# Split matmuls that run from the last column to the first, and logits of two heads in turn, in a decoder trunk

## The chip, the core and the metric

The kernel runs on one core of a Trainium2 chip. The metric is the device time of one execution in microseconds. The core has a matmul engine (TensorE, PE in the profile, with its weight loads shown apart as PEld), VectorE (DVE), ScalarE (ACT), GpSimd (POOL) and SyncE (SP), which here issues the large transfers from HBM.

## What is computed

A decoder trunk of two layers on 256 tokens of width 1024, all in float32. Layer 0 mixes by causal pooling, then a dense SwiGLU of width 2816. Layer 1 is a dilated sliding-window attention, then a top-2-of-8 expert SwiGLU of width 3584. Cut to what matters:

```python
h = h + pool_mixer(rmsnorm(h, a_norm[0]), a_proj[0], a_scale[0])
hn = rmsnorm(h, ffn_norm[0])
h = h + (silu(hn @ dense_w_gate) * (hn @ dense_w_up)) @ dense_w_down
kv = rmsnorm(h, kv_norm) @ w_kv                  # keys and values, 3 groups x 16 heads x 64
q = rmsnorm(h, b_norm[0]) @ w_q
logits = einsum('brnqhd,brnkhd->brnhqk', qs, kb) * HEAD_DIM ** -0.5 + bias   # per group, in its dilated window
...                                              # softmax over the three groups' keys together
h = h + merged @ w_o
xf = rmsnorm(h, ffn_norm[1])
...                                              # the two best of 8 experts for each token
ys = (silu(xb @ moe_w_gate[e]) * (xb @ moe_w_up[e])) @ moe_w_down[e]
h = h + gate * ys
return rmsnorm(h, final_norm)
```

## The kernel before

**Split matmuls.** Every large matmul takes float32 operands that are cut in two numbers of the type fp32r, a high part and a low part. ScalarE writes the high part `wh` of a weight piece as a copy to fp32r (line 178), VectorE subtracts it from the raw weights to give the low part `wl` (L182). The helper `mm3` then makes three matmuls for each 128 rows of the contraction: high by high and high by low (L190), and low by high (L193), all into one PSUM tile. With `weights_first` the weight piece is the stationary operand and 256 tokens are the moving one (gate, up and down of the dense layer, and the keys and queries). Without it the activations are stationary and the moving operand is a piece of the weights, 256 columns wide for the values and 512 for the output projection and the experts. The profile names the operands with the moving one first or last, by the program's names, and gives shapes as stationary and moving.

From the loops, the program runs 3312 split matmuls of 256 moving columns (1584 in the dense layer, 1728 for keys, queries and values) and 4104 of 512 (4008 in the experts, 96 in the output projection). The scatter of the experts' results (`scatter`, L1070 and L1071, 64 matmuls of 512 columns) uses fp32r operands too, but doesn't go through `mm3`. The last piece of the last expert (`native_unit`, L1042), the transposes, the gathers and the attention itself are plain float32 matmuls, each of which the profile shows as two records.

**Attention.** It runs in four blocks `b` of four heads. In each block come the projections of keys and queries, then the values, each cut into steps of 24 split matmuls. The queries and keys of a pair of heads, 2j and 2j+1, lie in one tile, the even head on partitions 0 to 63 and the odd one on 64 to 127. For each head `h` and each half `i` of the tokens (an item), `scores` makes four logits matmuls of 128 columns with a contraction of 64 (L615) into one PSUM bank, VectorE adds the bias, read backwards, and takes the maximum (L620), and ScalarE takes the exponential (L624). The probabilities are turned by TensorE one tick later (`transpose_probs`, L631).

**Order.** Everything is recorded in program order, and each engine runs its list in that order. `step` and `run` go through the projection steps. `later(n, fn)` puts other work n ticks later, a tick being one step. Items are started two to a tick, and the first tick after the queries takes four. In blocks 0 to 2 the list is (head 0, half 0), (0, 1), (1, 0), (1, 1), and so on, in block 3 all heads of half 0 come first. So the logits stand between the steps of the values projection (`ps_v`), on partitions that change from item to item only where the head changes.

Of the kernel before, what the change touches and what calls it, by code (L numbers as in the profile page):

```python
# [37 lines left out]
P = 128  # L38
# [57 lines left out]
def trunk(ctx, tc, x, a_norm, a_proj, a_scale, kv_norm, w_kv, b_norm, w_q, w_o, rel_bias,  # L96
          ffn_norm, w_gate, w_up, w_down, moe_router, moe_gate, moe_up, moe_down, final_norm,
          c_misc, c_band, c_onehot, c_mask, out):
    nc = tc.nc
# [26 lines left out]
    def bankB(name):  # L126
        return psB.tile([P, 512], F32, tag="b", name=name)
# [6 lines left out]
    def later(n, fn, rank=1):  # L134
        serial[0] += 1
        pending.append((clock[0] + n, rank, serial[0], fn))
# [33 lines left out]
    def split(raw, name):  # L170
# [11 lines left out]
            nc.vector.tensor_sub(lv, raw, hv.bitcast(F32))  # L182
        return hv, lv

    def mm3(o, terms, start, stop, weights_first):
        n = len(terms)
        for k, (wh, wl, xh, xl) in enumerate(terms):
            for m, xx in enumerate((xh, xl)):
                a, b = (wh, xx) if weights_first else (xx, wh)
                nc.tensor.matmul(o, a, b, start=start and k == 0 and m == 0, stop=False)  # L190
        for k, (wh, wl, xh, xl) in enumerate(terms):
            a, b = (wl, xh) if weights_first else (xh, wl)
            nc.tensor.matmul(o, a, b, start=False, stop=stop and k == n - 1)  # L193

    steps = []
    ahead = [2]
# [2 lines left out]
    def step(raw_of, cut, name, mm, post=None):  # L199
        steps.append((raw_of, cut, name, mm, post))  # L200
# [54 lines left out]
    def project(src, rows, xh, xl, outs, start, stop, name, post=None):  # L255
        u = unit(src, rows, 256, name)
        for j in range(2):
            def mm(wh, wl, j=j):
                mm3(outs(j), [(wh[:, k, :], wl[:, k, :], xh()[:, k, :], xl()[:, k, :]) for k in range(rows)],
                    start, stop, True)  # L260

            step(u, lambda raw, j=j: raw[:, :, j * P:(j + 1) * P], f"{name}_{j}", mm, post if j == 1 else None)
# [321 lines left out]
    kvT = {}  # L584
# [22 lines left out]

    SEG_KEYS = (((0, 1), (0, 0), (1, 0), (2, 0)), ((0, 0), (2, 1), (1, 1), (0, 1)))

    def scores(b, h, i, tb, sm):  # L610
        nm = f"{b}_{h}_{i}"
        j, q0 = h // 2, 64 * (h % 2)
        pl = bankB(f"ps_l{nm}")
        for s, (g, kt) in enumerate(SEG_KEYS[i]):
            nc.tensor.matmul(pl[:, s * P:(s + 1) * P], kvT["q", g][q0:q0 + 64, j, i * P:(i + 1) * P],  # L615
                             kvT["k", g][q0:q0 + 64, j, kt * P:(kt + 1) * P], start=True, stop=True)
        lg = av["at"].tile([P, 512], F32, tag="lg", name=f"lg{nm}", bufs=4)
        mx = av["at"].tile([P, 2], F32, tag="mx", name=f"mx{nm}", bufs=4)
        sl = slice(0, 4) if i == 0 else slice(4, 0, -1)
        nc.vector.tensor_tensor_reduce(out=lg.rearrange("p (s c) -> p s c", s=4),  # L620
                                       in0=pl.rearrange("p (s c) -> p s c", s=4), in1=tb[:, h, sl, ::-1],
                                       op0=ALU.add, op1=ALU.max, scale=1.0, scalar=-3e38, accum_out=mx[:, 0:1])
        nc.vector.tensor_scalar(mx[:, 1:2], mx[:, 0:1], -1.0, None, op0=ALU.mult)
        nc.scalar.activation(lg, lg, AF.Exp, bias=mx[:, 1:2], accum_out=sm[:, i, h:h + 1])  # L624
        return lg

    def transpose_probs(b, h, i, lg):
        nm = f"{b}_{h}_{i}"
        pt = bankB(f"ps_pT{nm}")
        for c in range(4):  # L630
            nc.tensor.transpose(pt[:, c * P:(c + 1) * P], lg[:, c * P:(c + 1) * P], ident)  # L631
        prT = st["late"].tile([P, 512], F32, tag="prT", name=f"prT{nm}")
        nc.scalar.activation(prT, pt, AF.Copy)
        return prT
# [27 lines left out]
    def out_proj(b, o):  # L662
        u = unit(w_o[b * 256:(b + 1) * 256, :], 2, D, f"o{b}")
        for n in range(2):
            def mm(wh, wl, n=n):
                oh, ol = o["o"]
                for i in range(2):
                    pw = bankA(f"ps_o{b}_{n}_{i}")
                    mm3(pw, [(wh[:, k, :], wl[:, k, :], oh[:, k, i * P:(i + 1) * P], ol[:, k, i * P:(i + 1) * P])
                             for k in range(2)], True, True, False)  # L670
                    hs = h2[:, i, n * 512:(n + 1) * 512]
                    nc.vector.tensor_add(hs, hs, pw)

            step(u, lambda raw, n=n: raw[:, :, n * 512:(n + 1) * 512], f"o{b}_{n}", mm)

    def items_of(b):
        if b == 3:
            return [(h, i) for i in range(2) for h in range(4)]
        return [(h, i) for h in range(4) for i in range(2)]


    def attention_block(b, prev):
        c0 = b * 256
        cur = {"b": b, "probs": {}}

        def begin():
            av["big"] = av["bigp"].tile([P, BIG], F32, tag="big", name=f"big{b}")
            cur["tb"] = bias_tile(b)
            cur["sm"] = av["at"].tile([P, 2, 4], F32, tag="sm", name=f"sm{b}")
            if prev is not None:  # L690
                def bank():
                    prev["U"] = bankB(f"ps_U{prev['b']}")

                later(1, bank)
                for n, (h, i) in enumerate(items_of(prev["b"])):
                    later(1 + n * 3 // 4, lambda h=h, i=i: attend(prev["b"], h, i, prev["probs"][h, i],
                                                                     prev["U"][:, i * T + h * 64:i * T + (h + 1) * 64]))
                def merge():
                    on, oh, ol = merge_tiles(prev["b"], av["one"])
                    prev["o"] = (oh, ol)  # L700
                    for i in range(2):
                        merged(prev["sm"], on, i, prev["U"][:, i * T:(i + 1) * T])
                        later(2, lambda i=i: turn_merged(prev["b"], on, oh, ol, i))

                later(8, merge)
# [33 lines left out]
            out_proj(prev["b"], prev)  # L739

        def start_scores():
            def do_scores(h, i):
                lg = scores(b, h, i, cur["tb"], cur["sm"])
                later(1, lambda: cur["probs"].__setitem__((h, i), transpose_probs(b, h, i, lg)), 0)

            for n, (h, i) in enumerate(items_of(b)):
                later(n // 2, lambda h=h, i=i: do_scores(h, i))

        then(start_scores)
        if b == 3:  # L750
# [5 lines left out]
        def values(g):  # L756
            v0 = 3 * D + g * D + c0
            u = unit(w_kv[:, v0:v0 + 256], NK, 256, f"v{b}_{g}")
            pv = {}

            def done():
                vv = av["ap"].tile([P, 2, T], F32, tag=f"v{g}", name=f"vv{b}_{g}")
                for i in range(2):
                    nc.scalar.activation(vv[:, i, :], pv[i][:, :T], AF.Copy, scale=st["pair"][0][:, i:i + 1])
                kvT["v", g] = vv
                if b == 3 and g == NG - 2:
                    big = av["big"] = av["bigp"].tile([P, BIG], F32, tag="big", name="big4")
                    nc.sync.dma_start(big[:, 4096:4096 + D], ffn_norm[1:2, :].to_broadcast([P, D]))
                    prefetch(RING, lambda name: big[:, :2048], lambda name: big[:, 2048:4096])
                if b == 3 and g == NG - 1:  # L770
                    prefetch(RING, slot(xp, "xH"), slot(xp, "xL"))

            for kh in range(2):
                def mm(wh, wl, kh=kh):
                    for i in range(2):
                        if kh == 0:
                            pv[i] = bankA(f"ps_v{b}_{g}_{i}")
                        ts = slice(i * P, (i + 1) * P)
                        mm3(pv[i][:, :T], [(wh[:, k, :], wl[:, k, :], ff["akH"][:, 4 * kh + k, ts],
                                            ff["akL"][:, 4 * kh + k, ts]) for k in range(4)],  # L780
                            kh == 0, kh == 1, False)

                step(u, lambda raw, kh=kh: raw[:, 4 * kh:4 * kh + 4, :], f"v{b}_{g}_{kh}", mm,
                     done if kh == 1 else None)
# [204 lines left out]
    def new_slots(e, sfx):  # L989
        m1 = mo["m1"]  # L990
        oh = m1.tile([P, 2, P], F32, tag="oh", name=f"oh{sfx}{e}")
        xeH = m1.tile([P, NK, P], F32R, tag="xeH", name=f"xeH{sfx}{e}")
        xeL = m1.tile([P, NK, P], F32R, tag="xeL", name=f"xeL{sfx}{e}")
        ohT = m1.tile([P, 2, P], F32R, tag=f"ohT{e % 2}", name=f"ohT{sfx}{e}")
        return oh, xeH, xeL, ohT
# [200 lines left out]
    with tc.If(top_count > P):  # L1196
        late = mo["mp"].tile([P, 2, NE], F32, name="late")
        nc.vector.tensor_scalar(late, mo["pos"], -float(P), None, op0=ALU.add)
        for e in range(NE):
            count = nc.values_load(cnt_i[0:1, e:e + 1], min_val=0, max_val=T)  # L1200
            with tc.If(count > P):
                g = new_slots(e, "o")
# [43 lines left out]
```

## Time and profile before

| | |
|---|---|
| median of 3 runs | 1545.69 us (1543.4 to 1547.26) |
| the profiled execution | 1544.2 us, of which 1542.4 us are the span from its first to its last instruction |
| TensorE busy | 1517.8 us, 98% of the span |
| VectorE busy | 1194.1 us, 77% |
| ScalarE busy | 1007.2 us, 65% |
| mean granted TensorE clock | 0.995 of 2.4 GHz |
| read from HBM | 438.36 MB, 285 GB/s over the span |

By time, the pooling takes the first 20 us or so, the dense layer runs to about 200 us, the attention to about 525 us, and the experts to about 1527 us. A busy matmul in the profile spans from its start to a modelled end, and the next one starts before that end; the pace of the engine is read from the distance of starts.

### The profile page before, as it was taken

How to read it: one execution, taken by the hardware profiler on the slowest of the kernel's cores; microseconds unless marked ns; L12 is line 12 of the kernel's file. 1: busy time of each engine (PE TensorE's matmuls, PEld its weight loads, DVE VectorE, ACT ScalarE, POOL GpSimd, SP SyncE). 2: the span in 40 equal slices, each digit the busy share in tenths (PEclk: the TensorE clock that was granted, in tenths of full speed). 3: DMA queues.
4: the chain of work that ended last, by engine and by line, in shares of the span. 5: the costliest groups of instructions: out<-in, count | busy, mean ns of one | idle time of the engine just before them, and what ended most of it. 6: DMA issues, size and time to landing. Idle time of an engine off the chain costs nothing. (4 is left out here: it accounts for less than half of the span.)

```text
span 1542.4 us, 22560 instructions
## 1 busy us (share of the span) xinstructions
PE 1517.8 (98%) x8849; PEld 1335.7 (87%) x8849; DVE 1194.1 (77%) x1346; ACT 1007.2 (65%) x1206; POOL 9.0 (1%) x16
## 2 busy tenths in 40 slices
PE   8999999999999999999999999999999999999996
PEld 7999999999999988888888888888888888888884
DVE  6666555454545589989989899989889998998984
ACT  5444445435353587878777777777777787877773
POOL 0000000000000000000000000000000000000001
PEclk9999999999999999999999999999999999999998
DMA  9955584647474789999999999999999999999931
GB/s 308 304 177 175 188 210 154 175 133 175 133 181 155 259 300 377 381 321 368 384 330 355 382 334 354 382 344 356 365 375 329 369 374 330 363 381 333 360 134 30
DMA packets 274803, 441.08 MB, mean 286 GB/s; under 512 B 28720, under 2 KB 100656, under 8 KB 274688
## 3 DMA queue, kind: packets, MB, share of 16 engines
q1 hardware_dynamic: 252448, 433.11, 79.7%
q10 hardware_dynamic: 22240, 6.45, 2.9%
q8 instruction: 71, 1.16, 0.3%
q14 instruction: 44, 0.36, 0.1%
HBM read 438.36 MB, written 1.17 MB: 285 GB/s over the span
## 5 line engine op out<-in xcount | busy, mean ns | idle before, releaser
L182 DVE TENSOR_TENSOR wl_mu<-raw_mu,wh_mu 128x1024 fp32r<-128x1024 f32 x196 | 232.4, 1222 | 35.6 <-ACT wh_mu L178 35.6
L182 DVE TENSOR_TENSOR wl_mg<-raw_mg,wh_mg 128x1024 fp32r<-128x1024 f32 x204 | 242.2, 1222 | 11.1 <-ACT wh_mg L178 10.1
L190 PE MATMUL ps_y<-wh_md,hid 128*128 128x512 f32 x880 | 237.2, 391 | 0.0
L178 ACT ACTIVATE wh_mg<-raw_mg 128x1024 fp32r<-128x1024 f32 x204 | 213.2, 1059 | 33.4 <-PE ps_y L190 24.6
L182 DVE TENSOR_TENSOR wl_md<-raw_md,wh_md 128x1024 fp32r<-128x1024 f32 x190 | 222.7, 1220 | 0.0
L178 ACT ACTIVATE wh_mu<-raw_mu 128x1024 fp32r<-128x1024 f32 x196 | 204.1, 1056 | 19.4 <-PE ps_mg L190 17.3
L178 ACT ACTIVATE wh_md<-raw_md 128x1024 fp32r<-128x1024 f32 x190 | 195.4, 1058 | 23.5 <-PE ps_mu L190 14.4
L190 PEld LDWEIGHTS ps_y<-wh_md,hid 128*128 128x128 f32 x880 | 164.1, 188 | 33.7 <-issue 0.5
L190 PE MATMUL ps_mg<-wh_mg,xeH 128*128 128x512 f32 x448 | 178.4, 398 | 0.0
L190 PE MATMUL ps_mu<-wh_mu,xeH 128*128 128x512 f32 x448 | 176.0, 393 | 0.0
L190 PE MATMUL ps_mg<-wh_mg,xeL 128*128 128x512 f32 x448 | 175.0, 391 | 0.0
L190 PE MATMUL ps_mu<-wh_mu,xeL 128*128 128x512 f32 x448 | 174.6, 390 | 0.0
L193 PE MATMUL ps_mg<-wl_mg,xeH 128*128 128x512 f32 x448 | 138.1, 390 | 0.0
L193 PE MATMUL ps_mu<-wl_mu,xeH 128*128 128x512 f32 x448 | 138.0, 389 | 0.0
L193 PE MATMUL ps_y<-wl_md,hid 128*128 128x512 f32 x440 | 135.8, 390 | 0.0
L193 PEld LDWEIGHTS ps_mg<-wl_mg,xeH 128*128 128x128 f32 x448 | 84.1, 188 | 18.1
L193 PEld LDWEIGHTS ps_mu<-wl_mu,xeH 128*128 128x128 f32 x448 | 84.1, 188 | 17.8
L190 PEld LDWEIGHTS ps_mu<-wh_mu,xeL 128*128 128x128 f32 x448 | 84.2, 188 | 17.0
L190 PEld LDWEIGHTS ps_mu<-wh_mu,xeH 128*128 128x128 f32 x448 | 84.1, 188 | 17.0
L190 PEld LDWEIGHTS ps_mg<-wh_mg,xeL 128*128 128x128 f32 x448 | 84.3, 188 | 16.3
L190 PEld LDWEIGHTS ps_mg<-wh_mg,xeH 128*128 128x128 f32 x448 | 84.2, 188 | 16.3
L193 PEld LDWEIGHTS ps_y<-wl_md,hid 128*128 128x128 f32 x440 | 82.6, 188 | 17.3
(244 smaller groups left out, 2712.7 us busy)
## 6 DMA issues: line engine op xcount, KB each, us to landing
raw_mg<-in_moe_w_gate_dram SPq DMA_DIRECT2D x102, 1024.0 KB, 7.1
raw_mu<-in_moe_w_up_dram SPq DMA_DIRECT2D x98, 1024.0 KB, 7.0
raw_md<-in_moe_w_down_dram SPq DMA_DIRECT2D x96, 1024.0 KB, 7.3
big<-in_moe_w_down_dram SPq DMA_DIRECT2D x16, 1024.0 KB, 7.5
big<-in_moe_w_up_dram SPq DMA_DIRECT2D x14, 1024.0 KB, 7.0
raw_k<-in_w_kv_dram SPq DMA_DIRECT2D x12, 1024.0 KB, 5.2
raw_q<-in_w_q_dram SPq DMA_DIRECT2D x12, 1024.0 KB, 5.4
raw_v<-in_w_kv_dram SPq DMA_DIRECT2D x12, 1024.0 KB, 5.4
```

The costliest lines, as they stand in the source:

```text
L178: nc.scalar.activation(hv, raw, AF.Copy)
L182: nc.vector.tensor_sub(lv, raw, hv.bitcast(F32))
L190: nc.tensor.matmul(o, a, b, start=start and k == 0 and m == 0, stop=False)
L193: nc.tensor.matmul(o, a, b, start=False, stop=stop and k == n - 1)
```

## The change

`mm3` calls a new helper `backward` in place of the matmul. It gives the moving operand and the output with a step of -1 over the columns, so that the last column is read first and written first. Each column still lands in its place; the numbers and the order of the matmuls are the same. The other matmuls, the scatter among them, stay as they were.

The logits matmuls move out of `scores` into `pair_logits`, which takes two PSUM banks at once and issues the four matmuls of the even head and the four of the odd head by turns. What follows for each head stays in `scores`. `pairs_of` gives the pairs of heads in order, one pair to a tick where two items were.

```diff
--- before.py
+++ after.py
@@ -182,15 +182,18 @@
             nc.vector.tensor_sub(lv, raw, hv.bitcast(F32))
         return hv, lv
 
+    def backward(o, a, b, start, stop):
+        nc.tensor.matmul(o[:, ::-1], a, b[:, ::-1], start=start, stop=stop)
+
     def mm3(o, terms, start, stop, weights_first):
         n = len(terms)
         for k, (wh, wl, xh, xl) in enumerate(terms):
             for m, xx in enumerate((xh, xl)):
                 a, b = (wh, xx) if weights_first else (xx, wh)
-                nc.tensor.matmul(o, a, b, start=start and k == 0 and m == 0, stop=False)
+                backward(o, a, b, start and k == 0 and m == 0, False)
         for k, (wh, wl, xh, xl) in enumerate(terms):
             a, b = (wl, xh) if weights_first else (xh, wl)
-            nc.tensor.matmul(o, a, b, start=False, stop=stop and k == n - 1)
+            backward(o, a, b, False, stop and k == n - 1)
 
     steps = []
     ahead = [2]
@@ -607,13 +610,17 @@
 
     SEG_KEYS = (((0, 1), (0, 0), (1, 0), (2, 0)), ((0, 0), (2, 1), (1, 1), (0, 1)))
 
-    def scores(b, h, i, tb, sm):
+    def pair_logits(b, j, i):
+        pls = [bankB(f"ps_l{b}_{2 * j + r}_{i}") for r in range(2)]
+        for s, (g, kt) in enumerate(SEG_KEYS[i]):
+            for r in range(2):
+                rows = slice(64 * r, 64 * r + 64)
+                nc.tensor.matmul(pls[r][:, s * P:(s + 1) * P], kvT["q", g][rows, j, i * P:(i + 1) * P],
+                                 kvT["k", g][rows, j, kt * P:(kt + 1) * P], start=True, stop=True)
+        return pls
+
+    def scores(b, h, i, pl, tb, sm):
         nm = f"{b}_{h}_{i}"
-        j, q0 = h // 2, 64 * (h % 2)
-        pl = bankB(f"ps_l{nm}")
-        for s, (g, kt) in enumerate(SEG_KEYS[i]):
-            nc.tensor.matmul(pl[:, s * P:(s + 1) * P], kvT["q", g][q0:q0 + 64, j, i * P:(i + 1) * P],
-                             kvT["k", g][q0:q0 + 64, j, kt * P:(kt + 1) * P], start=True, stop=True)
         lg = av["at"].tile([P, 512], F32, tag="lg", name=f"lg{nm}", bufs=4)
         mx = av["at"].tile([P, 2], F32, tag="mx", name=f"mx{nm}", bufs=4)
         sl = slice(0, 4) if i == 0 else slice(4, 0, -1)
@@ -673,11 +680,13 @@
 
             step(u, lambda raw, n=n: raw[:, :, n * 512:(n + 1) * 512], f"o{b}_{n}", mm)
 
+    def pairs_of(b):
+        if b == 3:
+            return [(j, i) for i in range(2) for j in range(2)]
+        return [(j, i) for j in range(2) for i in range(2)]
+
     def items_of(b):
-        if b == 3:
-            return [(h, i) for i in range(2) for h in range(4)]
-        return [(h, i) for h in range(4) for i in range(2)]
-
+        return [(2 * j + r, i) for j, i in pairs_of(b) for r in range(2)]
 
     def attention_block(b, prev):
         c0 = b * 256
@@ -739,12 +748,15 @@
             out_proj(prev["b"], prev)
 
         def start_scores():
-            def do_scores(h, i):
-                lg = scores(b, h, i, cur["tb"], cur["sm"])
-                later(1, lambda: cur["probs"].__setitem__((h, i), transpose_probs(b, h, i, lg)), 0)
-
-            for n, (h, i) in enumerate(items_of(b)):
-                later(n // 2, lambda h=h, i=i: do_scores(h, i))
+            def do_pair(j, i):
+                pls = pair_logits(b, j, i)
+                for r in range(2):
+                    h = 2 * j + r
+                    lg = scores(b, h, i, pls[r], cur["tb"], cur["sm"])
+                    later(1, lambda h=h, lg=lg: cur["probs"].__setitem__((h, i), transpose_probs(b, h, i, lg)), 0)
+
+            for n, (j, i) in enumerate(pairs_of(b)):
+                later(n, lambda j=j, i=i: do_pair(j, i))
 
         then(start_scores)
         if b == 3:
```
```

On TensorE, the first tick of logits in block 0, between two steps of the values projection. `ps_l_h_i` is the bank of the logits of head h and half i, `big` holds queries and keys. Before:

```order
L193 MATMUL ps_v_0_1_2872<-wl_v_0_0_2796,akH 128x256 x4
L615 MATMUL ps_l_0_0_2885<-big_2427 128x128 x4
L615 MATMUL ps_l_0_1_2895<-big_2427 128x128 x4
L615 MATMUL ps_l_1_0_2905<-big_2427 128x128 x4
L615 MATMUL ps_l_1_1_2915<-big_2427 128x128 x4
L190 MATMUL ps_v_0_0_2859<-wh_v_0_1_2824,akH 128x256
```

The same place in the change, where the first eight of sixteen matmuls of logits are shown:

```order
L186 MATMUL ps_v_0_1_2872<-wl_v_0_0_2796,akH 128x256 x4
L618 MATMUL ps_l_0_0_2885<-big_2427 128x128
L618 MATMUL ps_l_1_0_2886<-big_2427 128x128
L618 MATMUL ps_l_0_0_2885<-big_2427 128x128
L618 MATMUL ps_l_1_0_2886<-big_2427 128x128
L618 MATMUL ps_l_0_0_2885<-big_2427 128x128
L618 MATMUL ps_l_1_0_2886<-big_2427 128x128
L618 MATMUL ps_l_0_0_2885<-big_2427 128x128
L618 MATMUL ps_l_1_0_2886<-big_2427 128x128
L618 MATMUL ps_l_0_1_2905<-big_2427 128x128
```

The same sixteen matmuls now change the head, and with it the partitions, at every one of them. The split matmuls around them stand where they stood, now recorded by the helper's line L186.

On TensorE again, the second tick of logits in block 3, behind the transposes of the tick before (`ps_pT`), before:

```order
L631 MATMUL ps_pT_2_0_5338<-misc,lg_2_0_5281 128x128 x4
L631 MATMUL ps_pT_3_0_5345<-misc,lg_3_0_5291 128x128 x4
L615 MATMUL ps_l_0_1_5352<-big_4744 128x128 x4
L615 MATMUL ps_l_1_1_5362<-big_4744 128x128 x4
L190 MATMUL ps_v_1_0_5379<-wh_v_1_0_5226,akH 128x256
```

The same place in the change, up to the sixth of eight matmuls of logits:

```order
L638 MATMUL ps_pT_2_0_5338<-misc,lg_2_0_5286 128x128 x4
L638 MATMUL ps_pT_3_0_5345<-misc,lg_3_0_5291 128x128 x4
L618 MATMUL ps_l_0_1_5352<-big_4744 128x128
L618 MATMUL ps_l_1_1_5353<-big_4744 128x128
L618 MATMUL ps_l_0_1_5352<-big_4744 128x128
L618 MATMUL ps_l_1_1_5353<-big_4744 128x128
L618 MATMUL ps_l_0_1_5352<-big_4744 128x128
L618 MATMUL ps_l_1_1_5353<-big_4744 128x128
```

In block 3 the items of one tick were already of two heads, four matmuls each; now the head changes at every matmul here too.

## Rows read from the trace of the kernel before

**Rows 1.** First part of the page: busy time, share of the span, instructions of each engine.

```profile
PE 1517.8 (98%) x8849; PEld 1335.7 (87%) x8849; DVE 1194.1 (77%) x1346; ACT 1007.2 (65%) x1206; POOL 9.0 (1%) x16
```

**Rows 2.** Windows: stretch, its length, busy us of engines, granted clock, DMA share, GB/s.

```profile
56.00:180.00 124.00, 124.00 (x1025) 122.63 (x1024) 79.21 (x87) 54.53 (x67) 0.00 (x0) 1.00 0.59 192
255.00:333.00 78.00, 76.81 (x637) 75.39 (x636) 36.26 (x58) 34.58 (x54) 0.00 (x0) 1.00 0.56 158
...
487.00:525.00 38.00, 38.00 (x322) 36.54 (x321) 20.36 (x41) 20.47 (x39) 0.00 (x0) 1.00 0.55 199
560.00:1500.00 940.00, 940.00 (x4371) 782.00 (x4370) 853.00 (x852) 726.04 (x788) 0.00 (x0) 1.00 0.97 350
```

**Rows 3.** Waits of TensorE between 255 and 525 us: total us, times, longest.

```profile
PE ps_k L190 <- ACT wh_k L178: 2.0, 2, 1.2
```

**Rows 4.** Waits of SP's queue over the whole span, the longest.

```profile
SPq L163 <- DVE wl_mg L182: 311.2, 107, 18.4
```

**Rows 5.** Timeline, block 0 (start us, us): logits, partly from their 3rd and 13th record.

```profile
261.20 3.50 PE L615 MATMUL ps_l<-big 64*128 64x128 f32 x32
264.63 0.39 PE L190 MATMUL ps_v<-wh_v,akH 128*128 128x256 f32 x1
...
269.45 2.05 PE L615 MATMUL ps_l<-big 64*128 64x128 f32 x16
269.77 1.72 PE L615 MATMUL ps_l<-big 64*128 64x128 f32 x14
270.89 0.61 PE L615 MATMUL ps_l<-big 64*128 64x128 f32 x4
271.43 0.39 PE L190 MATMUL ps_v<-wh_v,akH 128*128 128x256 f32 x1
```

**Rows 6.** Timeline of TensorE, block 3: logits and what follows.

```profile
492.38 2.82 PE L615 MATMUL ps_l<-big 64*128 64x128 f32 x32
495.13 0.39 PE L190 MATMUL ps_v<-wh_v,akH 128*128 128x256 f32 x1
...
499.94 1.71 PE L615 MATMUL ps_l<-big 64*128 64x128 f32 x16
501.58 0.38 PE L190 MATMUL ps_v<-wh_v,akH 128*128 128x256 f32 x1
```

**Rows 7.** Timeline, block 0, after its first logits: VectorE, ScalarE and TensorE.

```profile
264.89 0.68 DVE L620 CUSTOM_DVE_ANT_0 lg<-ps_l,big 128x512 f32<-128x512 f32 x1
...
266.43 0.19 ACT L624 ACTIVATION_READ_ACCUMULATOR lg<-lg,mx 128x1 f32 x1
...
267.61 1.91 PE L631 MATMUL ps_pT<-misc,lg 128*128 128x128 f32 x16
```

**Rows 8.** Groups of VectorE: count, busy us, mean ns of one, idle before.

```profile
L620 DVE CUSTOM_DVE_ANT_0 lg<-ps_l,big 128x512 f32<-128x512 f32 x16 | 11.0, 689 | 1.3 <-PE ps_l L615 1.2
L620 DVE CUSTOM_DVE_ANT_1 lg<-ps_l,big 128x512 f32<-128x512 f32 x16 | 11.0, 688 | 14.8 <-PE ps_l L615 14.8
...
L726 DVE TENSOR_TENSOR big<-ps_k,rb_a 128x512 f32<-128x512 f32 x12 | 8.2, 688 | 21.7 <-PE ps_k L193 21.7
```

**Rows 9.** Timeline of TensorE, split matmuls of 256 and of 512 columns.

```profile
100.53 1.12 PE L193 MATMUL ps_g<-xfH,wl_g 128*128 128x256 f32 x8
...
101.49 0.28 PE L190 MATMUL ps_g<-xfH,wh_g 128*128 128x256 f32 x1
...
900.35 1.07 PE L190 MATMUL ps_y<-wh_md,hid 128*128 128x512 f32 x4
901.26 0.61 PE L193 MATMUL ps_y<-wl_md,hid 128*128 128x512 f32 x2
901.71 1.07 PE L190 MATMUL ps_y<-wh_md,hid 128*128 128x512 f32 x4
```

**Rows 10.** Timeline of TensorE, plain float32 of 512 columns: all records, and the last.

```profile
1515.49 3.59 PE L1042 MATMUL ps_y<-big,hid 128*128 128x512 f32 x8
1518.49 0.59 PE L1042 MATMUL ps_y<-big,hid 128*128 128x512 f32 x1
```

## Prediction

> **What bounds the kernel now.** The page's first part comes first: TensorE is busy for 98% of the span, no other engine for more than 77% [rows 1]. A busy share says little of pipelined matmuls, so the windows and the waits come next. In the dense layer, the attention and the experts, TensorE is busy all the time but for a us or two, at a granted clock of 1.00 [rows 2], and in the 270 us from 255 to 525 us it waits for another engine twice, 2.0 us in all [rows 3]. VectorE and ScalarE have work for about half of the attention and for 853 and 726 of 940 us in the experts [rows 2]. The transfers wait too: SP's queue stands still until VectorE has read a raw buffer, 311.2 us for the gate pieces alone [rows 4], so HBM isn't the limit even at 350 GB/s. TensorE's own pace sets the time nearly everywhere: what it gains or loses per matmul goes into the total almost whole.
>
> The timeline gives the pace, from start to start. Eight split matmuls of 256 columns go from 100.53 to 101.49, 120 ns each; six of 512 from 900.35 to 901.71, 226.7 ns each [rows 9]. At 2.4 GHz, the level at which the clock stands [rows 2], 256 columns pass in 106.7 ns and 512 in 213.3, so a split matmul costs 13.3 ns beyond its columns in either size. A plain float32 matmul is two records of two column-times each: seven intervals from 1515.49 to 1518.49 are 428.6 ns each [rows 10], 1.9 ns beyond 1024 column-times.
>
> **The change part by part.** It adds and removes no instruction. It has two parts.
>
> *The logits.* A run of 16 records (two items) takes 1.98 us from its start to the next split matmul, at 0.112 us a record, ten of them from 269.77 to 270.89 [rows 5]. So 16 × 0.112 = 1.79, and 0.19 goes to the way in and out. In block 0 all 16 are of one head, on the same 64 partitions. In block 3, where the two items are of two heads, the same 16 take 1.64 us (499.94 to 501.58) [rows 6], the time of (1.64 − 0.19) / 0.112 = 13 records: at the change of the head three records of one run beside the other. In the 32 of block 0's first tick, (3.43 − 0.19) / 0.112 = 28.9 slots are taken, three saved at its one change of partitions [rows 5]; in the 32 of block 3, with three changes, 22.9, nine saved [rows 6]. So heads on different halves of the partitions do run side by side, where the engine has both at hand. With a change at every matmul I take all records in twos: 8 slots for 16 records, 0.19 + 8 × 0.112 = 1.09 us, and 16 slots for 32, 1.98 us.
>
> Block 0 has one tick of 32 and two of 16, and so have blocks 1 and 2: 1.45 + 2 × 0.89 = 3.23 us each, 9.7 for the three. Block 3 saves 2.75 − 1.98 = 0.77 and 2 × (1.64 − 1.09) = 1.10, 1.9 us. Together 11.6 us.
>
> Does the gain stay? Behind the logits, VectorE and ScalarE work item by item. Today ScalarE ends the fourth exponential at 266.43 + 0.19 = 266.62 and TensorE turns the first probabilities at 267.61 [rows 7]. The change brings that to 267.61 − 1.45 = 266.16. VectorE starts when the first bank is full; the even head fills at the pace it had, only with the odd one beside it, so that start stays, and VectorE's steps stay as long as they are (0.69 us for the large one [rows 8]). The fourth exponential then still ends at about 266.6, and its transposes are the last of four groups in 1.91 us: they start at 266.16 + 3/4 × 1.91 = 267.6, 1 us later than needed. If that cover were gone (a weight split of ScalarE ahead of an exponential), a tick would lose up to the 1 us it saved. I take no loss; the bounds of this part are −11.6 us and, if records of two heads no longer overlap at all, the slots saved today: 3 × 3.1 + 9.1 + 2 × 3 = 24.4 × 0.112 = +2.7 us.
>
> The Trainium skill, "TensorEngine Tiling (Array Packing)", section "Key Properties", says that tiles of the array operate independently and that a change of the tiling mode, unlike a change of tile, drains the engine. The 0.19 us in and out and the overlap inside agree with it; by it the sum would be the same.
>
> *The backward operands.* Nothing on TensorE reads backwards today, so this has no price in the trace. From below: at best the 13.3 ns shrink to the plain records' 1.9, 11.4 × (3312 + 4104) = 84.5 us saved. From above: a backward column could cost two column-times, as each record of a plain matmul does: 428.6 − 226.7 = 201.9 for 4104 matmuls and, with 2 × 106.7 + 1.9 = 215.2, 215.2 − 120 = 95.2 for 3312, +1144 us. The nearest row that reads backwards is VectorE's: L620 takes 128 × 512 logits and a bias with a step of −1 in 688 to 689 ns, and L726, a product of the same size from PSUM with all operands forward, 688 [rows 8]. Direction costs nothing there. The columns, the contiguous span and the banks stay the same, and as all matmuls of a chain are turned alike, the distance in time between two visits to a column does too. I take 0.
>
> The sum against the profiled execution: 1544.2 − 11.6 = 1532.6 us (its span from 1542.4 to 1530.8, with 1.8 around it). The median of the runs is 1.5 us above that execution, so 1545.7 − 11.6 = 1534 us is the forecast.
>
> **The rivals.**
>
> *Backward is quicker.* The 13.3 ns are no matter of columns, since they are the same for 256 and 512, nor of weights, which plain records load as well. They come with fp32r streaming, and an order of reading could change them. For it speaks only that there is something to gain. Against it: nothing shows that the extra hangs on the direction. Whole, it gives 1534 − 84.5 = 1449.5 us; VectorE would stand that, with the expert window 46 us shorter (4008 × 11.4 ns) and its 853 us in 894. Half of it gives 1492.
>
> The Trainium skill, "TensorE: Matmul & The Clock Gate", section "Back-to-back issue gap", gives N/2.4 + 2.5 ns for isolated warm matmuls, an estimate of 215.8 and 109.2 ns here. The trace differs by 11 ns in both sizes, so split matmuls aren't what that rule describes.
>
> *Backward is slower.* The place is each of 7416 matmuls, so a small price decides: 11.6 us / 7416 = 1.6 ns, four column-times, and the change loses what the logits gain; 2.2 ns more than cancels it by 0.3%. One more lot of 13.3 ns would give 1534 + 98.6 = 1633 us, two column-times a column 2678. The pairs of VectorE's rows speak against it, on another engine.
>
> *The logits don't overlap* when the head changes each time, the backward part being free: 1545.7 to 1548.4 us. Block 3 speaks against it, with the shortest run where the head changes most.
>
> **How the numbers follow.** I give 0.52 to the forecast, 0.26 to a quicker backward, 0.16 to a slower one, 0.06 to logits without a gain. The forecast's own range, with a stall of the cover or a little more overlap, is 1528 to 1542. From 1452 to 1548 it takes in nearly all of the quicker case and the logits without a gain, and leaves out the slower one, whose prices have no near end, and some 2% below. About 0.3% (4.6 us) is what a measurement of this kernel can tell from no change: faster holds the forecast and the quicker case, less a little where exponentials come late, 0.77; same is 0.07; slower 0.16.
>
> **What would show it.** In the profile after, the logits of block 0 should go from 3.43 and 1.98 us to about 1.98 and 1.09, and block 3's to the same. Six backward matmuls of 512 columns should take 1.36 us, eight of 256 0.96; the scatter's, which stay forward, are the measure beside them in the same trace. TensorE should not begin to wait for ScalarE between 255 and 525 us. The prediction is wrong if the distance of split matmuls moves by 2 ns or more in either direction, if the logits keep their length, or if the time so saved comes back as a wait for the exponentials or the weight splits.

## The result, and the profile after

The changed kernel takes 1554.18 us (median of five runs, 1553.60 to 1556.05) beside 1545.69 us before (five runs, 1543.40 to 1547.65): a ratio of 1.0057, 95% interval 1.0042 to 1.0071. It is 0.6% slower. The forecast was 1534 us with a range up to 1548; the case that came true is the rival called backward is slower.

The page and the windows of the kernel after, in the same stretches as [rows 1] and [rows 2]; in a window's row the stretch's length is followed by busy us of TensorE, its weight loads, VectorE, ScalarE and GpSimd, then granted clock, DMA share and GB/s:

```profile
PE 1529.4 (99%) x8849; PEld 1322.2 (85%) x8849; DVE 1196.8 (77%) x1346; ACT 1005.4 (65%) x1206; POOL 8.6 (1%) x16
...
255.00:333.00 78.00, 76.95 (x662) 74.55 (x662) 39.29 (x63) 33.21 (x52) 0.00 (x0) 1.00 0.58 159
560.00:1500.00 940.00, 940.00 (x4263) 763.66 (x4262) 835.42 (x817) 707.62 (x767) 0.00 (x0) 1.00 0.96 345
```

No instruction more, the clock still at 1.00, TensorE busy as before. But the two long stretches have moved in opposite directions. From 255 to 333 us, with the logits and matmuls of 256 columns, TensorE gets through 662 records where it did 637; from 560 to 1500 us, the experts, through 4263 where it did 4371, and there VectorE and ScalarE are less busy as well, because less work reaches them. In that stretch TensorE has no idle time, before or after: its matmuls themselves are slower.

The timeline of TensorE after, at the places of [rows 9] (start us, us, then the instruction; the pace is the distance of two starts over the count between them):

```profile
101.59 1.11 PE L186 MATMUL ps_g<-xfH,wl_g 128*128 128x256 f32 x8
102.54 0.28 PE L186 MATMUL ps_u<-xfH,wh_u 128*128 128x256 f32 x1
...
900.94 1.10 PE L186 MATMUL ps_y<-wh_md,hid 128*128 128x512 f32 x4
...
902.34 1.10 PE L186 MATMUL ps_y<-wh_md,hid 128*128 128x512 f32 x4
```

Eight matmuls of 256 columns take 102.54 - 101.59 = 0.95 us, 119 ns each (120 before); the series of 20 among the experiments puts it at 118.5. Six of 512 take 902.34 - 900.94 = 1.40 us, 233.3 ns each (226.7 before). The plain float32 matmuls of the last piece (L1054 now), which stay forward, take 3.59 us for eight as in [rows 10].

The scatter, which the prediction names as the measure beside them, is another group: fp32r matmuls among the experts' split ones, still forward. Their row before and after (count, least, median and longest ns of one, first and last start in us):

```profile
L1070 PE MATMUL ps_z<-y,ohT x32: 389/389/793, 667.0 to 1527.9; 128*128 128x512 f32 x32
```

```profile
L1082 PE MATMUL ps_z<-y,ohT x32: 397/399/793, 655.7 to 1538.1; 128*128 128x512 f32 x32
```

They did not stand still. The same instruction takes 10 ns more by its modelled duration; from its start to the next, most took 226 or 227 ns before and take 238 or 239 now. With the logits alone changed the median is 389 again, with the experts' reads alone backward (and their writes forward) 399. So a forward matmul between backward ones slows too, and the paces measured here belong to the stream as a whole, not to each turned matmul by itself.

The logits, in block 0, from the timeline of TensorE (what follows each run is shown with it), and the weight loads of the second run alone, with the wait ahead of each in brackets:

```profile
257.46 2.06 PE L618 MATMUL ps_l<-big 64*128 64x128 f32 x32
259.44 0.39 PE L186 MATMUL ps_v<-wh_v,akH 128*128 128x256 f32 x1
...
264.25 1.64 PE L618 MATMUL ps_l<-big 64*128 64x128 f32 x16
265.83 0.39 PE L186 MATMUL ps_v<-wh_v,akH 128*128 128x256 f32 x1
...
269.74 1.16 PE L618 MATMUL ps_l<-big 64*128 64x128 f32 x16
270.83 0.39 PE L186 MATMUL ps_v<-wh_v,akH 128*128 128x256 f32 x1
```

```profile
264.25 0.29 PEld L618 LDWEIGHTS ps_l<-big 64*128 64x128 f32 x2 [0.19 <-ACT prT L640]
264.74 0.96 PEld L618 LDWEIGHTS ps_l<-big 64*128 64x128 f32 x14 [0.19 <-ACT prT L640]
```

The 32 records now take 1.98 us, the last 16 take 1.09. The 16 in the middle take 1.58: its first even record goes at 264.25, the rest 0.49 us later.

Over the whole attention, from 255 to 525 us, the logits' weight loads wait 1.5 us in 8 times for that releaser, ScalarE's copy of transposed probabilities out of PSUM (`prT`); before, it was 0.7 us in 4 times.

### The profile page after: what moved, and what is told of

The parts are those of the page before. It is cut to its first block, busy times and chain, and to the rows that moved or that the text cites. A ratio compares the mean times of both kernels' runs of the same rounds, so it can differ in the third digit from the quotient of the medians.

```text
span 1552.4 us, 22567 instructions
## 1 busy us (share of the span) xinstructions
PE 1529.4 (99%) x8849; PEld 1322.2 (85%) x8849; DVE 1196.8 (77%) x1346; ACT 1005.4 (65%) x1206; POOL 8.6 (1%) x16
## 3 DMA queue, kind: packets, MB, share of 16 engines
q8 instruction: 71, 1.16, 0.3%
## 5 line engine op out<-in xcount | busy, mean ns | idle before, releaser
L182 DVE TENSOR_TENSOR wl_mu<-raw_mu,wh_mu 128x1024 fp32r<-128x1024 f32 x196 | 233.1, 1219 | 41.3 <-ACT wh_mu L178 41.3
L182 DVE TENSOR_TENSOR wl_mg<-raw_mg,wh_mg 128x1024 fp32r<-128x1024 f32 x204 | 243.8, 1220 | 14.6 <-ACT wh_mg L178 13.6
L186 PE MATMUL ps_y<-wh_md,hid 128*128 128x512 f32 x880 | 243.1, 399 | 0.0
L178 ACT ACTIVATE wh_mg<-raw_mg 128x1024 fp32r<-128x1024 f32 x204 | 213.0, 1058 | 38.9 <-PE ps_y L186 21.6
L182 DVE TENSOR_TENSOR wl_md<-raw_md,wh_md 128x1024 fp32r<-128x1024 f32 x190 | 222.9, 1217 | 1.0 <-ACT wh_md L178 1.0
L178 ACT ACTIVATE wh_mu<-raw_mu 128x1024 fp32r<-128x1024 f32 x196 | 203.9, 1055 | 23.5 <-PE ps_mg L186 23.0
L178 ACT ACTIVATE wh_md<-raw_md 128x1024 fp32r<-128x1024 f32 x190 | 195.2, 1057 | 30.0 <-PE ps_mu L186 19.4
L186 PEld LDWEIGHTS ps_y<-wh_md,hid 128*128 128x128 f32 x880 | 164.3, 188 | 39.0 <-issue 0.5
L186 PE MATMUL ps_mg<-wh_mg,xeH 128*128 128x512 f32 x448 | 181.5, 405 | 0.0
L186 PE MATMUL ps_mu<-wh_mu,xeH 128*128 128x512 f32 x448 | 179.4, 400 | 0.0
L186 PE MATMUL ps_mu<-wh_mu,xeL 128*128 128x512 f32 x448 | 178.0, 397 | 0.0
L186 PE MATMUL ps_mg<-wh_mg,xeL 128*128 128x512 f32 x448 | 178.0, 397 | 0.0
L186 PE MATMUL ps_mu<-wl_mu,xeH 128*128 128x512 f32 x448 | 141.3, 397 | 0.0
L186 PE MATMUL ps_mg<-wl_mg,xeH 128*128 128x512 f32 x448 | 141.3, 397 | 0.0
L186 PE MATMUL ps_y<-wl_md,hid 128*128 128x512 f32 x440 | 138.8, 397 | 0.0
L186 PEld LDWEIGHTS ps_mg<-wl_mg,xeH 128*128 128x128 f32 x448 | 84.2, 188 | 20.4
L186 PEld LDWEIGHTS ps_mu<-wl_mu,xeH 128*128 128x128 f32 x448 | 84.2, 188 | 20.3
L186 PEld LDWEIGHTS ps_mu<-wh_mu,xeL 128*128 128x128 f32 x448 | 84.3, 188 | 19.7
L186 PEld LDWEIGHTS ps_mu<-wh_mu,xeH 128*128 128x128 f32 x448 | 84.2, 188 | 19.6
L186 PEld LDWEIGHTS ps_mg<-wh_mg,xeL 128*128 128x128 f32 x448 | 84.4, 188 | 18.6
L186 PEld LDWEIGHTS ps_mg<-wh_mg,xeH 128*128 128x128 f32 x448 | 84.3, 188 | 18.5
L186 PEld LDWEIGHTS ps_y<-wl_md,hid 128*128 128x128 f32 x440 | 82.7, 188 | 20.0
```

The source lines that it names most:

```text
L178: nc.scalar.activation(hv, raw, AF.Copy)
L186: nc.tensor.matmul(o[:, ::-1], a, b[:, ::-1], start=start, stop=stop)
```

## The experiments

My theory after the result: the logits gain what block 0 shows, some 10 us; backward saves about 1.6 ns at 256 columns and costs 6.6 ns at 512, and nothing else moved. The rivals: backward slows both sizes a little; or the alternating logits lose their gain elsewhere and the backward part is small. All diffs are against the changed kernel unless said otherwise, and each ratio is to runs of the kernel before on the same chip.

**Halves of the change.** The logits alone:

```diff
-        nc.tensor.matmul(o[:, ::-1], a, b[:, ::-1], start=start, stop=stop)
+        nc.tensor.matmul(o, a, b, start=start, stop=stop)
```

> The logits of two heads by turns, all split matmuls forward again. Theory (the two parts act apart, each by TensorE's own pace): in the trace of the change the logits take 18.6 us where they took 28.2, so 1545.7 - 9.6 = 1536 us, ratio 0.994. Rival (what the logits gain comes back as waits later, or the turns themselves slow the work behind them): 1545 us or more, ratio 1.0 or above.

Measured: 1535.27 us, ratio 0.9936 (0.9924 to 0.9948). The backward operands alone, as a diff against the kernel before (the third matmul of `mm3` likewise, and no other line):

```diff
-                nc.tensor.matmul(o, a, b, start=start and k == 0 and m == 0, stop=False)
+                nc.tensor.matmul(o[:, ::-1], a, b[:, ::-1], start=start and k == 0 and m == 0, stop=False)
```

> All split matmuls backward, the logits as before. Theory (parts act apart): the measured 1554.2 us without the 9.6 us of the logits, 1564 us, ratio 1.012; matmuls of 512 columns 233.3 ns apart, of 256 columns 118.4. Rival (backward costs only where something else changed with it): below 1556 us, ratio under 1.007.

Measured: 1563.04 us, ratio 1.0117 (1.0103 to 1.0132). And the whole change, but backward only at 256 columns:

```diff
-        nc.tensor.matmul(o[:, ::-1], a, b[:, ::-1], start=start, stop=stop)
+        if b.shape[-1] == 256:
+            o, b = o[:, ::-1], b[:, ::-1]
+        nc.tensor.matmul(o, a, b, start=start, stop=stop)
```

> Logits by turns; split matmuls of 256 columns backward, those of 512 forward. Theory (the loss hangs on the 512 columns alone, and the backward 256 are a small gain of 1.6 ns each): 1554.2 - 4104 x 6.6 ns = 1527 us, ratio 0.988, and 5 us below the run with the logits alone. Rival (the pace of the experts' matmuls is set by something else in the change): the experts stay at 233 ns and the time above 1545 us.

Measured: 1530.42 us, ratio 0.9906 (0.9893 to 0.9919), 3 us above what was expected, on the theory's side. The three steps by these medians: the logits -10.1 us (1545.4 to 1535.3), backward at 256 columns -4.9 (1535.3 to 1530.4, 1.5 ns for each of 3312 matmuls), backward at 512 +23.8 (1530.4 to 1554.2, 5.8 ns for each of 4104). That they add up to +8.8 us, near the +8.5 of the change, is no test, since each step starts where the one before ends. The run with the backward operands alone is one: +17.7 us (1545.4 to 1563.0), and with the -10.1 of the logits alone +7.6, so the parts act apart to within about a us.

The experts' share can be read by itself, from the first to the last load of the experts' gate weights (`ps_mg<-wh_mg,xeH`). After, that is 1510.0 - 527.7 = 982.3 us; with backward at 256 columns only, 1485.8 - 527.6 = 958.2. The difference, 24.1 us, is 6.0 ns for each of their 4008 matmuls.

**Which of the two operands.** Two kernels that turn only one of them in the experts (256 columns turned as in the change, the output projection forward). Only the write:

```diff
+        if expert:
+            nc.tensor.matmul(o[:, ::-1], a, b, start=start, stop=stop)
```

> Logits by turns, 256 columns backward; in the experts the matmuls of 512 columns only write backward and read forward, so that the experts' columns are mixed up. Theory (the read sets the pace): the experts keep 227 ns and the time is that of the run with the 256 columns alone backward, 1530 us, ratio 0.990. Rival (the write sets it): 1554 us, ratio 1.005.

Measured: 1530.26 us, ratio 0.9901 (0.9884 to 0.9917). Only the read:

```diff
+        if expert:
+            nc.tensor.matmul(o, a, b[:, ::-1], start=start, stop=stop)
```

> The same with the matmuls of 512 columns in the experts reading backward and writing forward (the experts' columns are mixed up). Theory (the read sets the pace): 233 ns in the experts, 1530.4 + 4008 x 5.8 ns = 1554 us, ratio 1.005. Rival (the write sets it): 1530 us, ratio 0.990.

Measured: 1555.43 us, ratio 1.0061 (1.0044 to 1.0078). The timeline of the experts, write backward first, then read backward:

```profile
892.13 1.07 PE L187 MATMUL ps_y<-wh_md,hid 128*128 128x512 f32 x4
...
893.49 1.07 PE L187 MATMUL ps_y<-wh_md,hid 128*128 128x512 f32 x4
```

```profile
893.19 1.10 PE L187 MATMUL ps_y<-wh_md,hid 128*128 128x512 f32 x4
...
894.59 1.10 PE L187 MATMUL ps_y<-wh_md,hid 128*128 128x512 f32 x4
```

Six take 1.36 us with the write backward, the forward pace, and 1.40 with the read backward. In the experts, all of the price is in the read.

**The pace by itself.** A kernel of nothing but series of split matmuls, 24 each, back to back, on operands whose rows lie 520 columns apart:

```diff
+    series('p512_ff_', 512, 'f', 'f', 0)
+    series('p512_bb_', 512, 'b', 'b', 0)
+    series('p512_rb_', 512, 'b', 'f', 0)
+    series('p512_wb_', 512, 'f', 'b', 0)
```

> No trunk at all (the output is zeros): series of 24 split matmuls by themselves, nothing else at work, each into one bank; p..ff both operands forward, bb both backward, rb only the read backward, wb only the write, alt forward and backward by turns, at 128 to 512 columns; a, b, c with the moving operand shifted by 1, 2 and 4 columns. Theory 1 (the read sets it): rb at 512 columns 233 ns apart and wb 227. Theory 2 (the write sets it): wb 233 and rb 227. Theory 3 (it needs the traffic of the other engines): all 227 at 512 and 120 at 256. A price per column would give 230 at 384 columns minus 3.3 for each 128 fewer, a fixed one the same 6.6 ns at each size; the 118.4 ns at 256 columns speak for neither, so that the sizes between are open.

Its timeline, a series a row (ff forward, bb backward, rb only the read, wb only the write):

```profile
17.54 5.72 PE L124 MATMUL p_ff__123<-mv,wt 128*128 128x512 f32 x24
23.10 5.80 PE L124 MATMUL p_bb__149<-mv,wt 128*128 128x512 f32 x24
28.74 5.80 PE L124 MATMUL p_rb__175<-mv,wt 128*128 128x512 f32 x24
34.38 5.71 PE L124 MATMUL p_wb__201<-mv,wt 128*128 128x512 f32 x24
39.92 5.72 PE L124 MATMUL p_alt__227<-mv,wt 128*128 128x512 f32 x24
45.48 3.02 PE L124 MATMUL p_ff__253<-mv,wt 128*128 128x256 f32 x24
```

From row to row, 24 take 5.56, 5.64, 5.64 and 5.54 us: again the read decides, and it does so with nothing else at work. Forward and backward by turns (alt) take 5.56, no more than all forward: again a backward matmul doesn't pay a price of its own. In the other sizes of this kernel backward is slower by 1.6 ns at 128 columns and 1.7 at 448 and quicker by 2.9 at 320 and 0.8 at 384, so the price is neither fixed nor one per column. And forward is 231.7 ns here, not 226.7, though nothing else runs: where the operands lie matters too. So a second such kernel takes the trunk's layout (rows 512 columns apart), and then varies the stationary operand's columns and the place at which the moving one begins:

```diff
+    series('walkf', 512, 'f')
+    series('colszf', 512, 'f', 32)
+    series('shbf', 512, 'f', shift=1, times=16)
```

> No trunk (the output is zeros): series of split matmuls by themselves, with the operands laid out as in the trunk (rows of 512 columns); f and b at a name's end is the moving operand and the output forward or backward. Walk: as in the trunk, 512 and then 256 columns. Cols: 512 moving columns with 96, 64 and 32 stationary columns (x, y, z). Sh a to j: one moving operand of 512, its start shifted by 0, 1, 2, 3, 4, 8, 16, 32, 64, 128 columns; ws a to g: the stationary one shifted by 1, 2, 4, 8, 16, 32, 64; two: the stationary one with a step of 2. Theory (the read of the moving operand meets the load of the next weights in SBUF): what a matmul takes beyond its 213.3 ns falls with the stationary columns, to a quarter at 32 of them, and changes with the shifts. Rival (a fixed start of an fp32r matmul): 13.3 ns forward whatever the stationary columns and the shifts. Walk should show the trunk's 227 and 233 ns at 512, 120 and 118 at 256.

```profile
17.92 4.70 PE L126 MATMUL walkf<-mv,wt 128*128 128x512 f32 x20
22.45 4.83 PE L126 MATMUL walkb<-mv,wt 128*128 128x512 f32 x20
27.12 2.56 PE L126 MATMUL walkf<-mv,wt 128*128 128x256 f32 x20
29.52 2.53 PE L126 MATMUL walkb<-mv,wt 128*128 128x256 f32 x20
31.89 4.76 PE L126 MATMUL colsxf<-mv,wt 128*96 128x512 f32 x20
...
50.43 4.79 PE L126 MATMUL colszf<-mv,wt 128*32 128x512 f32 x20
55.05 4.83 PE L126 MATMUL colszb<-mv,wt 128*32 128x512 f32 x20
59.72 3.81 PE L126 MATMUL shaf<-wide,wtw 128*128 128x512 f32 x16
63.36 3.90 PE L126 MATMUL shab<-wide,wtw 128*128 128x512 f32 x16
67.10 3.96 PE L126 MATMUL shbf<-wide,wtw 128*128 128x512 f32 x16
70.89 3.94 PE L126 MATMUL shbb<-wide,wtw 128*128 128x512 f32 x16
...
134.36 3.89 PE L126 MATMUL wsaf<-wide,wtw 128*128 128x512 f32 x16
138.09 3.90 PE L126 MATMUL wsab<-wide,wtw 128*128 128x512 f32 x16
```

The first four rows give the trunk's paces: 4.53 / 20 = 226.5 and 233.5 ns at 512 columns, 120 and 118.5 at 256. If the extra time went with the length of the weight load, a quarter of the stationary columns (colsz) should bring forward to about 217 ns and backward to 218; it makes forward worse, 4.62 / 20 = 231, and leaves backward at 233.5. If each way had its fixed start, shifting the moving operand by one column should change nothing; forward goes from 3.64 / 16 = 227.5 (shaf) to 3.79 / 16 = 236.9 (shbf). Both ideas fall as they were put. That the read meets the weight load in another way is not ruled out: shifting the stationary operand alone by one column takes forward to 3.73 / 16 = 233.1 (wsaf), and by 64 columns back to 227.5.

**What in the order of the read.** The read in blocks of columns, either with each block turned in its place (in) or with the blocks in reverse order (out); the write stays forward:

```diff
+            if outer == "b":
+                m = m[:, ::-1, :]
+            if inner == "b":
+                m = m[:, :, ::-1]
```

> No trunk (the output is zeros): series of split matmuls by themselves, 512 and then 256 columns, laid out as in the trunk, all writing forward. one f and b: the whole read forward and backward (227 and 233 ns at 512). in a to g: blocks of 2, 4, 8, 16, 32, 64, 128 columns in order, each read backward inside; out a to g: the blocks read in reverse order, each forward inside. Theory 1 (what counts is the direction of single columns, within short blocks): in a and b 233, out b and all longer ones 227. Theory 2 (what counts is the direction of the long sweep, so how the read moves against the other streams): in with short blocks 227, out with short blocks 233, the two changing places towards blocks of 64 to 128. Theory 3 (only the column at which the read starts or ends counts): all in rows alike, all out rows alike.

The timeline; the letters a to g are blocks of 2, 4, 8, 16, 32, 64 and 128 columns:

```profile
28.31 4.71 PE L124 MATMUL ina<-mv,wt 128*128 128x512 f32 x20
32.86 4.83 PE L124 MATMUL outa<-mv,wt 128*128 128x512 f32 x20
...
56.08 5.50 PE L124 MATMUL ind<-mv,wt 128*128 128x512 f32 x20
61.41 4.84 PE L124 MATMUL outd<-mv,wt 128*128 128x512 f32 x20
...
89.29 4.71 PE L124 MATMUL outg<-mv,wt 128*128 128x512 f32 x20
93.84 2.56 PE L124 MATMUL onef<-mv,wt 128*128 128x256 f32 x20
...
108.12 2.43 PE L124 MATMUL inc<-mv,wt 128*128 128x256 f32 x20
110.39 2.56 PE L124 MATMUL outc<-mv,wt 128*128 128x256 f32 x20
```

Pairs turned in place cost next to nothing (227.5), and so do blocks of 128 in reverse order (4.55 / 20 = 227.5). What lies between decides: 16 columns turned in place cost 5.33 / 20 = 266.5 ns. At 256 columns, blocks of 8 turned in place are quicker than forward, 2.27 / 20 = 113.5. So theories 1 and 3 fall. At 512 columns theory 2 holds for the blocks in reverse order, which change over at blocks of 64; in blocks turned in place the change comes at 8 columns already, and nothing in it foresaw the 266.5 at 16. A second set takes orders that keep each four columns (16 bytes) as they are and change only the order of these groups (turn: groups of a block reversed; skip: every hth group first; kips: the same with the rounds reversed):

```diff
+        if way == "turn":
+            return ap.rearrange("p (a g c) -> p a g c", c=4, g=size // 4)[:, :, ::-1, :]
+        if way == "skip":
+            return ap.rearrange("p (g h c) -> p h g c", c=4, h=size)
```

> No trunk (the output is zeros): series of split matmuls by themselves, 512 and then 256 columns, read and write in the same order. in: blocks of 8 and 16 (c, d) backward inside; both: blocks backward and the columns inside too, which is the whole backward; turn: within 8, 16, 32 columns the groups of four backward, the four forward; skip: every 2nd, 4th, 8th, 16th group of four, then the next; kips: the same, the last of these rounds first. Theory (only the order of the groups of four columns counts, not the order in a group): turn with 8 and 16 has the pace of in with 8 and 16 (233 and 267 ns at 512, 113 and 133 at 256). Rival (the step between columns counts): turn and in differ. Whether any order beats 226.7 ns at 512 is open.

```profile
56.49 5.49 PE L132 MATMUL turnd<-mv,wt 128*128 128x512 f32 x20
61.82 4.84 PE L132 MATMUL turne<-mv,wt 128*128 128x512 f32 x20
...
90.73 4.61 PE L132 MATMUL kipsb<-mv,wt 128*128 128x512 f32 x20
95.19 4.91 PE L132 MATMUL kipsc<-mv,wt 128*128 128x512 f32 x20
99.94 5.81 PE L132 MATMUL kipsd<-mv,wt 128*128 128x512 f32 x20
105.58 2.56 PE L132 MATMUL f<-mv,wt 128*128 128x256 f32 x20
```

Reversing groups inside 16 columns (turnd) costs the same 266.5 ns as reversing the columns. So, at one place and in a series by itself, the order of the 16-byte groups sets the pace: 223 ns for kipsb, which takes every fourth group first and the rounds in reverse, and 282 for kipsd, which does so with every sixteenth. In this set the write takes the same order as the read. For blocks turned in place that makes no difference (266.5 ns at 16 columns with the write either way); for skip and kips the two were not told apart.

**Better orders in the kernel.** Three kernels put them to use: blocks of 8 at 256 columns, with 512 forward; then kipsb at 512, with 256 backward; then skipb (every fourth group) at 256, with 512 forward.

```diff
+        if b.shape[-1] == 256:
+            o, b = (v.rearrange("p (a c) -> p a c", c=8)[:, :, ::-1] for v in (o, b))
```

> Logits by turns, 512 columns forward; the matmuls of 256 columns read and write each 8 columns backward, the blocks of 8 in order. Theory (the pace of a split matmul hangs on the order in which its read takes the groups of 16 bytes, by itself and in the trunk): 113.35 ns as in the series alone, so 1535.3 - 3312 x 6.65 ns = 1513 us, ratio 0.979. Rival (in the trunk the weight pieces or the traffic of the other engines hold the pace): 118 to 120 ns, 1530 to 1535 us.

Measured: 1530.79 us, ratio 0.9907 (0.9893 to 0.9920), a miss by 18 us. The timeline says why: the gates of the dense layer first, then queries.

```profile
100.81 1.12 PE L188 MATMUL ps_g<-xfH,wl_g 128*128 128x256 f32 x8
101.77 0.28 PE L188 MATMUL ps_g<-xfH,wh_g 128*128 128x256 f32 x1
...
243.13 1.07 PE L188 MATMUL ps_q<-aqH,wl_q 128*128 128x256 f32 x8
244.03 0.28 PE L188 MATMUL ps_q<-aqH,wh_q 128*128 128x256 f32 x1
```

The same instruction keeps 120 ns in the gates (0.96 / 8) and 112.5 in these queries (0.90 / 8): this order has two paces in the trunk, and most matmuls stay at the slower one; some 500 of 3312, all of queries and values, are at 113 or 114 ns. Why these is open.

```diff
+        else:
+            o, b = (v.rearrange("p (g h c) -> p h g c", c=4, h=4)[:, ::-1, :, :] for v in (o, b))
```

> Logits by turns, 256 columns backward; the matmuls of 512 columns read and write every fourth group of four columns, the last of the four rounds first, each forward. Theory (the order of the groups sets the pace in the trunk as in the series alone): 222.2 ns, so 1530.4 - 4104 x 4.4 ns = 1512 us, ratio 0.979. Rival (as with the blocks of 8, the trunk falls into another pace than the series): 227 to 233 ns, 1530 to 1555 us.

Measured: 1515.89 us, ratio 0.9807 (0.9790 to 0.9824), the fastest of all, 1.9% under the kernel before. Its experts:

```profile
925.94 1.05 PE L190 MATMUL ps_y<-wh_md,hid 128*128 128x512 f32 x4
...
927.27 1.05 PE L190 MATMUL ps_y<-wh_md,hid 128*128 128x512 f32 x4
```

Six take 1.33 us, 221.7 ns each. Against 1530.42 us, with 512 columns forward and 256 backward as here, the order saves 14.5 us, 3.5 ns for each of 4104 matmuls, 4 us less than was expected.

```diff
+        if b.shape[-1] == 256:
+            o, b = (v.rearrange("p (g h c) -> p h g c", c=4, h=4) for v in (o, b))
```

> Logits by turns, 512 columns forward; the matmuls of 256 columns read and write every fourth group of four columns, round by round. Theory: 113.2 ns as in the series alone, so 1535.3 - 3312 x 6.7 ns = 1513 us, ratio 0.979. Rival (the trunk falls into another pace): 117 to 120 ns, 1525 to 1535 us.

Measured: 1523.41 us, ratio 0.9855 (0.9840 to 0.9871), between the two cases that were expected: (1535.27 - 1523.41) / 3312 = 3.6 ns less than forward. This order and the one at 512 columns were not put into one kernel.

## Why the prediction was wrong

**What bounds the kernel** was right, and so the price of one step decided all: TensorE's own pace sets the time, before and after.

**The backward operands** are the step that failed: "I take 0". It rested on VectorE's reversed read [rows 8], a row of another engine, and on a free choice between far bounds. On TensorE the direction of the read changes the pace in both sizes, with opposite sign: 1.5 ns less at 256 columns and 5.8 more at 512 by the times, -4.9 and +23.8 us, +18.9 together. The write's direction, which the prediction treated together with the read, costs nothing. The scatter was to stand still as the measure beside the turned matmuls; it slowed with them, the first of its two matmuls mostly by about 11 ns. The rival that came true had its break-even right, 1.6 ns on the mean of 7416 matmuls: the mean is 18.9 / 7416 = 2.5 ns. That the price could differ between the sizes was not considered.

Its argument for a quicker backward, that the 13.3 ns beyond the columns hang on the order of reading, was nearer the truth than the chosen step: other orders gave back part of them, 221.7 ns at 512 columns. The Trainium skill, "TensorE: Matmul & The Clock Gate", section "Back-to-back issue gap", gives N/2.4 + 2.5 ns for isolated warm matmuls, an estimate of 215.8 at 512 columns: no order measured here reaches it.

**The logits** were right in mechanism and 2 us too large. Records of two heads do run in twos: 32 in 1.98 us and the last 16 in 1.09, both as forecast. The second run of a block takes 1.58 instead of 1.09. There the odd head needs its bank of PSUM with the second record; before, the second item of a run came to its bank eight records of 0.112 us later, 0.9 us. ScalarE still copies the transposed probabilities out of it, a bank every 0.49 us or so (four copies take 2.03). Four blocks at 0.49 are 2 us: -11.6 becomes -9.6, beside -10.1 by the times. The prediction named a wait on ScalarE as a way to fail, but for the exponentials and the weight splits, not for a bank.

**The cover** for the exponentials held: TensorE's waits from 255 to 525 us name ScalarE's weight splits and its copies out of PSUM, and no exponential.

**The sum** in its form holds: -9.6 us for the logits, -1.6 x 3312 = -5.3 and +6.6 x 4104 = +27.1 by the paces give +12 against a measured +8.5. The paces of the short stretches overstate the loss at 512 columns, since the experts as a whole lose 6.0 ns a matmul.

## What to carry to other kernels

A change of the access pattern on TensorE's moving operand can have a price, which no other engine's rows give: measure it in each size before it goes into thousands of matmuls, first in a series and then in the kernel, since an order that took 113.5 ns in a series kept 120 in most of the kernel. A group of matmuls that the edit leaves alone is no fixed point to measure against where it runs between the edited ones. Where an engine is busy throughout, a part of one or two per cent per instruction outweighs a local gain, and an edit that joins two parts is to be tried in halves. A run made shorter by working on two items at once needs both items' buffers at its start.

## What the runs showed of the hardware

The pace of split matmuls depends on the order in which the moving operand's 16-byte groups are read: from 223 to 282 ns at 512 columns and from 113 to 138 at 256 in the series, with the granted clock at its full level, 2.4 GHz. Order inside 16 bytes and, in the sizes tried, the order of blocks of 64 columns or more change it by 1.5 ns at most. Several paces are the columns plus a multiple of 16 column-times: 120.0 ns is 256 + 32 of them, 226.7 is 512 + 32, 233.3 is 512 + 48, 113.3 is 256 + 16. It is no rule: 223 ns is 512 + 23, and 118.5 is 256 + 28. Where the operands begin matters as well, the stationary one's place too (forward at 512 columns: 226.5 ns, 231.7 with rows 520 columns apart, 236.9 with the moving operand one column on, 233.1 with the stationary one), and one order has two paces in one kernel, 120 and 112.5 ns. A matmul's pace also hangs on its neighbours: the forward scatter went from 227 to 238 ns between backward matmuls.

What makes these steps is open: the length of the weight load and a fixed start per direction were tried and fell, and no other cause was shown.
